# All two-operand additions and subtractions of the second norm, the token combinations and the up weights on VectorE instead of partly on GpSimd

## The chip, the cores and the metric

The kernel runs on one core of a Trainium2 chip. The metric is the device time of one execution in microseconds (us). A core has five engines that each run their own queue of instructions in order: TensorE (PE in the profile, with its weight loads as PEld), VectorE (DVE), ScalarE (ACT), GpSimd (POOL) and SyncE (SP, which here issues DMAs).

## What is computed

One layer of a streaming encoder on 1088 tokens of width 1024 (1024 of a new stream, 64 of a running one). Only its end matters here:

```python
    x = x + gate1 * (jnp.concatenate([a_out, b_out], axis=-1) @ w_out)
    h2 = rms_norm(x, g_norm2) * (1 + scale2) + shift2
    x = x + gate2 * (jnp.square(jax.nn.relu(h2 @ w_up)) @ w_down)
    return x, latent_new, krope_new, s_new
```

`w_up` is 1024 x 4096, `w_down` 4096 x 1024, everything is float32.

## The kernel before, in words

Every float32 product is made of three products of rounded halves: `split(hi, lo, src, eng)` lets ACT copy `src` into a rounded `hi` and then lets `eng` compute `lo = src - hi` (line 102); `mm3` (lines 92 to 95) multiplies hi by hi, lo by hi and hi by lo. `sub` (line 105) is a subtraction on the engine named. A `split` or a `sub` costs one instruction with two operands in SBUF on the engine named.

The up and the down projection use a seven-product scheme (Strassen's) on halves of the tokens and halves of the width, so sums and differences of the token blocks `X[11]`, `X[12]`, `X[21]`, `X[22]` (128 x 4 x 544 each) and of the weight blocks are formed and split first. The 1088 tokens come in four chunks of 272 in the order `WORDER`, two halves (`HALVES`) of each of two token blocks.

The stretch that the change touches has these parts, in the order of time:

- Output projection (`main`, about 611 to 718 us): for each chunk of 272 tokens eight blocks `m` of 24 matmuls. For each `m` DVE adds the gated product to `x` (line 1323), ACT squares it (line 1330), and POOL adds the square to the chunk's sum `acc` (line 1331). The last chunk's sum is the tile `last`.
- Second norm (`norm2`, beside `main`, its last chunk beside the up projection): TensorE sums `acc` over the partitions (line 1345), DVE and POOL form the reciprocal root (lines 1348 and 1349), DVE a diagonal (line 1352), TensorE broadcasts it (line 1356), then per row block `k` DVE scales `x` (line 1362; its second operand is in PSUM) and ACT adds the shift (line 1364). After `k == 3` in the second token block, POOL subtracts `X[21]` from `X[11]` (line 1366, shown in the trace under line 105). Chunks of the first token block are split (`AH[0]` with POOL, `AH[1]` with DVE); for the second block `sums_of` forms three more sums, on POOL (lines 1262 to 1264).
- Token operands (`tokens`): `second` forms `X[22] - X[11]` into `ts` and splits it, `third` splits `X[11]`, then the operands 4, 5 and 6 are split. Four of the eight splits of `third`, and half of the sixteen for 5 and 6, have their subtraction on POOL, the others on DVE.
- Up weights (`weights`): for each of 16 column blocks `j`, `first` and `rest` form seven operands; `put(j, i, src, eng)` takes the next of ten slots, waits until the product that used it is done, and splits into it. For `j < 2` several of these, and for every `j` the seventh (`put(j, 6, ...)`), have their subtraction on POOL.
- Up projection (`up`, about 718 to 1060 us): `product(j, i, h)` runs 12 matmuls with weight operand `i` of block `j` and the half `h` of token operand `i`. Its result is copied out by ACT (line 1565) or added by DVE (line 1551); these free the PSUM bank.

`interleave` fixes by hand-written times in which order the streams are written out. When the program is built, a planner then puts the instructions of each engine in one fixed order, which need not be that of the source. On the chip each engine takes its instructions in that order, and one that waits holds up those behind it.

Of the kernel before, what the change touches and what calls it, by code (L numbers as in the profile page):

```python
# [71 lines left out]
def layer(ctx: ExitStack, tc: tile.TileContext, I, O):  # L72
# [31 lines left out]
    def sub(out, a, b, eng):  # L104
        eng.tensor_tensor(out=out, in0=a, in1=b, op=ALU.subtract)  # L105
# [1151 lines left out]
            return h, HALVES[0], ((0, 512 * h, HW, 0),)  # L1257
        return h, HALVES[1], ((0, 512 * h + HW, 512 - HW, 0), (1, SEQ + 32 * h, 32, 512 - HW))

    def sums_of(hs, eng=None):  # L1260

        POOL.tensor_tensor(out=X[21][:, :, hs], in0=X[21][:, :, hs], in1=X[22][:, :, hs], op=ALU.add)
        sub(X[12][:, :, hs], X[12][:, :, hs], X[22][:, :, hs], eng or POOL)
        POOL.tensor_tensor(out=X[12][:, :, hs], in0=X[12][:, :, hs], in1=X[11][:, :, hs], op=ALU.add)

    with ExitStack() as octx:
        ow = octx.enter_context(tc.tile_pool(reuse_waits="tile", name="ow", bufs=1))
# [12 lines left out]
        def main():  # L1280
            ld = {}

            def load(c):
                h, hs, parts = place(c)
                mx = [xw.tile([P, 4, HW], F32, name="mx") for _ in range(2)]
                for _, t0, n, o in parts:
                    SP.dma_start(mx[0][:, :, o:o + n], mix_d[:, 0:4, t0:t0 + n])
                    SP.dma_start(mx[1][:, :, o:o + n], mix_d[:, 4:8, t0:t0 + n])
                ld[c] = mx

            def load_x(c):
                h, hs, _ = place(c)
                for b in range(2):
                    tc.keep_in_program_order(SP.dma_start(
                        X[10 * (h + 1) + 1 + b][:, :, hs],
                        I["xo_T"][512 * b:512 * b + 512, c * HW:(c + 1) * HW].rearrange("(k p) n -> p k n", p=P)))

            for w, c in enumerate(WORDER):
                _, _, parts = place(c)
                if w == 0:  # L1300
                    mh, ml = mixh[1]
                else:
                    mx = ld.pop(c)
                    mh, ml = mix_pair() if w == 2 else [xw.tile([P, 8, HW], F32R, name=f"m{x}1", bufs=1) for x in "hl"]
                    split(mh[:, 0:4], ml[:, 0:4], mx[0], DVE)
                    split(mh[:, 4:8], ml[:, 4:8], mx[1], DVE)
                load_x(c)
                if w + 1 < 4:
                    load(WORDER[w + 1])
                acc = last[:, 0:HW] if w == 3 else nw.tile([P, HW], F32, name="acc")  # L1310
                for m in range(8):
                    yield 600, 0, has(f"wo {m}")
                    if w == 0 and m < len(early):
                        po = early[m]
                    else:
                        po = (g_bank if w == 0 and m < 6 else mm_bank)()[:, 0:HW]
                        for kt in range(KT):
                            n, o = wo_place(m, kt)
                            mm3(po, wo[n][0][:, o], wo[n][1][:, o], mh[:, kt], ml[:, kt], kt == 0, kt == KT - 1)
                            yield 340, 0, None  # L1320
                    x2 = rows_of(c, m)
                    for s, _, n, o in parts:
                        DVE.scalar_tensor_tensor(out=x2[:, o:o + n], in0=po[:, o:o + n], scalar=modT[:, 2, m, s:s + 1],
                                                 in1=x2[:, o:o + n], op0=ALU.mult, op1=ALU.add)
                    SP.dma_start(x2_d[:, m, c * HW:(c + 1) * HW], x2)
                    if m == 0:
                        ACT.activation(acc, x2, AF.Square)
                    else:
                        sq = nw.tile([P, HW], F32, name="sq", bufs=3)
                        ACT.activation(sq, x2, AF.Square)  # L1330
                        POOL.tensor_tensor(out=acc, in0=acc, in1=sq, op=ALU.add)
                sums[c] = acc
                done.add(f"x2 {c}")

        def norm2():
            for c in WORDER:
                h, hs, parts = place(c)
                end = c == WORDER[-1]
                yield 0, 0, has("up" if end else f"x2 {c}")
                yield 0, 2500, None  # L1340
                acc = sums.pop(c)
                blocks = ((0, P), (P, P), (2 * P, HW - 2 * P))
                pm = tp_bank()
                for j, (o, n) in enumerate(blocks):
                    PE.matmul(pm[:n, j:j + 1], lhsT=acc[:, o:o + n], rhs=ones[:, 0:1], start=True, stop=True)
                st = last[:, 272:275] if end else nw.tile([P, 3], F32, name="st")
                for a, b, n in ((0, 2, P), (2, 3, blocks[2][1])):
                    DVE.tensor_scalar(out=st[:n, a:b], in0=pm[:n, a:b], scalar1=1.0 / D, scalar2=EPS, op0=ALU.mult, op1=ALU.add)
                    POOL.tensor_tensor(out=st[:n, a:b], in0=st[:n, a:b], in1=mhalf[:n, 0:b - a], op=ALU.pow)
                dg = last[:, 288:672].rearrange("p (j t) -> p j t", j=3) if end else nw.tile([P, 3, P], F32, name="dg", bufs=1)  # L1350
                for j, (o, n) in enumerate(blocks):
                    DVE.tensor_scalar(out=dg[:n, j, :n], in0=ident[:n, :n], scalar1=st[:n, j:j + 1], scalar2=None, op0=ALU.mult)
                yield 0, 3000, None
                bc = tp_bank()
                for j, (o, n) in enumerate(blocks):
                    PE.matmul(bc[:, o:o + n], lhsT=ones[:n, :], rhs=dg[:n, j, :n], start=True, stop=True)
                yield 600, 300, None
                for k in range(8):
                    x = rows_of(c, k)
                    for s, _, n, o in parts:  # L1360
                        xs = x[:, o:o + n]
                        DVE.scalar_tensor_tensor(out=xs, in0=xs, scalar=G12[:, 1, k, s:s + 1], in1=bc[:, o:o + n],
                                                 op0=ALU.mult, op1=ALU.mult)
                        ACT.activation(xs, xs, AF.Identity, bias=modT[:, 3, k, s:s + 1])
                    if h == 1 and k == 3:
                        sub(X[11][:, :, hs], X[11][:, :, hs], X[21][:, :, hs], POOL)
                if h == 0:
                    split(AH[0][:, :, hs], AL[0][:, :, hs], X[11][:, :, hs], POOL)
                    split(AH[1][:, :, hs], AL[1][:, :, hs], X[12][:, :, hs], DVE)
                elif not end:  # L1370
                    sums_of(hs)
            done.add("norm2")
# [15 lines left out]
    with ExitStack() as uctx:  # L1388
# [27 lines left out]
        def tokens():  # L1416
# [11 lines left out]

            def third(h, cs):
                for k in range(4):  # L1430
                    part(3, X[11][:, k, cs], k, cs, POOL if k % 2 or False else DVE)
                yield 0, 500, None
                done.add(f"tokens 3 {h}")

# [2 lines left out]
            yield 0, 500, has("third 1", "norm2")  # L1437
            yield from second(1, HALVES[1])
            yield from third(1, HALVES[1])
            sums_of(HALVES[1], DVE)  # L1440
            AL[4] = keep.tile([P, 4, HT], F32R, name="al4", tag="x11")
            for j, x in ((4, 22), (5, 21), (6, 12)):
                for h, cs in enumerate(HALVES):
                    for k in range(4):
                        part(j, X[x][:, k, cs], k, cs, POOL if j > 4 and (k + h) % 2 else DVE)
                    done.add(f"tokens {j} {h}")
                    yield 0, 500, None
                if j < 6:
                    AL[j + 1] = apool.tile([P, 4, HT], F32R, name=f"al{j + 1}", tag=f"x{x}")
                else:  # L1450
                    more = keep.tile([P, 4, 4, P], F32R, name="wq_more", tag=f"x{x}")
                    slots.extend(((more[:, 0], more[:, 1]), (more[:, 2], more[:, 3])))
# [5 lines left out]
        def weights():  # L1458
# [11 lines left out]
            def first(j):  # L1470
# [3 lines left out]
                    raws[f] = t[:, 0:4], t[:, 4:8]  # L1474
                yield 0, 2500, None
                warr[j] = {}
                yield from put(j, 0, raws[j][0], POOL if j < 2 else DVE)
                yield from put(j, 1, raws[j][1], DVE)

            def rest(j):  # L1480
                (b11, b21), (b12, b22) = raws.pop(j), raws.pop(j + 16)
                t2 = tq.tile([P, 512], F32, name="tw").rearrange("p (k n) -> p k n", k=4)
                sub(b11, b12, b11, DVE)
                sub(t2, b22, b11, POOL if j < 2 else DVE)
                yield from put(j, 2, t2, DVE)
                yield 0, 1500, None
                if j >= 2:
                    yield from put(j, 5, b11, DVE)
                    yield 0, 1500, None
                sub(b12, b22, b12, DVE)  # L1490
                yield from put(j, 3, b12, POOL if j < 2 else DVE)
                done.add(f"third {j}")
                yield 0, 1500, None
                if j < 2:
# [1 line left out]
                sub(t2, b21, t2, DVE)  # L1496
                yield from put(j, 4, t2, DVE)
                yield 0, 1500, None
                yield from put(j, 6, b22, POOL)
                yield 0, 1500, None  # L1500

            yield from first(0)
# [340 lines left out]
```

## Time and profile before

| | us |
|---|---|
| median of 3 runs | 1420.18 (1418.73 to 1422.01) |
| the profiled execution, its own time | 1419.29 |
| span of that profile | 1417.5 |
| PE busy | 1349.8 (95% of the span) |
| DVE busy | 873.6 (62%) |
| ACT busy | 655.6 (46%) |
| POOL busy | 273.1 (19%) |

Busy time of an engine is a mean over very different stretches, so the rows further down are taken by stretch. In the rows of groups the number after the bar is the busy time of the group and the mean of one instruction in ns, and after the second bar the idle time in front of it and what ended it. In a timeline, a row gives its start, its length, the engine, the line, and in brackets the idle time before it; several neighbouring instructions of one kind are merged into one row (x8), and lengths of neighbours overlap a little, since an instruction ends after the next has begun. The granted clock is 1.00 where TensorE runs at 2.4 GHz and 0.50 at 1.2 GHz.

### The profile page before, as it was taken

How to read it: one execution, taken by the hardware profiler on the slowest of the kernel's cores; microseconds unless marked ns; L12 is line 12 of the kernel's file. 1: busy time of each engine (PE TensorE's matmuls, PEld its weight loads, DVE VectorE, ACT ScalarE, POOL GpSimd, SP SyncE). 2: the span in 40 equal slices, each digit the busy share in tenths (PEclk: the TensorE clock that was granted, in tenths of full speed). 3: DMA queues.
4: the chain of work that ended last, by engine and by line, in shares of the span. 5: the costliest groups of instructions: out<-in, count | busy, mean ns of one | idle time of the engine just before them, and what ended most of it. 6: DMA issues, size and time to landing. Idle time of an engine off the chain costs nothing.

```text
span 1417.5 us, 26453 instructions
## 1 busy us (share of the span) xinstructions
PE 1349.8 (95%) x10014; PEld 1263.6 (89%) x10014; DVE 873.6 (62%) x1894; ACT 655.6 (46%) x1623; POOL 273.1 (19%) x388
## 2 busy tenths in 40 slices
PE   6988899988999999999987999999999999999998
PEld 5888788886866778899986999999999999999998
DVE  5678777336455665654489665665544776774554
ACT  5455454335335566653455544444444333333332
POOL 3155445213121211013564000000000000000000
PEclk9999999999999999999998999999999999999999
DMA  9320021384243442164224534444437864533440
GB/s 347 109 72 9 16 72 55 107 235 129 84 142 123 157 120 71 44 204 135 80 76 125 182 132 140 156 140 131 141 113 271 324 221 152 185 114 108 127 126 33
DMA packets 165594, 188.17 MB, mean 133 GB/s; under 512 B 16814, under 2 KB 116442, under 8 KB 165466
## 3 DMA queue, kind: packets, MB, share of 16 engines
q1 hardware_dynamic: 158010, 180.90, 40.0%
q10 hardware_dynamic: 7456, 5.57, 1.2%
q8 instruction: 79, 1.29, 0.4%
q14 instruction: 49, 0.40, 0.1%
HBM read 132.97 MB, written 53.46 MB: 132 GB/s over the span
## 4 chain that ended last, share of the span: by engine, by line
PE 77%; DVE 10%; DMA 4%; POOL 3%; ACT 3%; issue 2%; SPq 0%; DVEq 0%; POOLq 0%; ACTq 0%
PE mm L93 13%; PE mm L94 13%; PE mm L95 13%; PE g L93 6%; PE g L95 6%; PE g L94 5%; PE mm L964 3%; PE tp L93 3%; PE tp L95 3%; PE tp L94 3%; PE g L991 2%; PE mm L166 2%; DMA raw<-in_w_in 1%; PE tp L1001 1%; DMA gv<-mix_d 1%
## 5 line engine op out<-in xcount | busy, mean ns | idle before, releaser
L101 ACT CAST opers<-quad 128x512 fp32r<-128x512 f32 x112 | 69.4, 620 | 184.6 <-PE mm L95 145.3
L102 DVE TENSOR_TENSOR opers<-quad,opers 128x512 fp32r<-128x512 f32 x112 | 77.1, 689 | 112.6 <-ACT opers L101 112.6
L93 PE MATMUL mm<-ah,wh 128*128 128x272 f32 x424 | 123.0, 291 | 6.2 <-ACT st L1565 6.2
L93 PE MATMUL mm<-opers 128*128 128x272 f32 x448 | 128.6, 287 | 0.3 <-DVE e L1775 0.3
L95 PE MATMUL mm<-opers 128*128 128x272 f32 x448 | 128.9, 288 | 0.0
L94 PE MATMUL mm<-opers 128*128 128x272 f32 x448 | 128.3, 286 | 0.0
L95 PE MATMUL mm<-ah,wl 128*128 128x272 f32 x424 | 122.7, 290 | 1.0 <-POOL wl L102 1.0
L94 PE MATMUL mm<-al,wh 128*128 128x272 f32 x424 | 122.8, 290 | 0.0
L93 PE MATMUL mm<-hh,wh 128*128 128x384 f32 (+2 forms) x264 | 90.6, 346 | 0.6 <-ACT hh L101 0.5
L94 PE MATMUL mm<-hl,wh 128*128 128x384 f32 (+2 forms) x264 | 87.6, 333 | 0.0
L95 PE MATMUL mm<-hh,wl 128*128 128x384 f32 (+2 forms) x264 | 87.2, 331 | 0.0
L93 PEld LDWEIGHTS mm<-ah,wh 128*128 128x128 f32 x424 | 81.2, 192 | 6.5 <-ACT st L1565 6.4
L93 PEld LDWEIGHTS mm<-opers 128*128 128x128 f32 x448 | 84.6, 189 | 0.5 <-issue 0.5
L95 PEld LDWEIGHTS mm<-opers 128*128 128x128 f32 x448 | 84.3, 188 | 0.0
L94 PEld LDWEIGHTS mm<-opers 128*128 128x128 f32 x448 | 84.1, 188 | 0.0
L95 PEld LDWEIGHTS mm<-ah,wl 128*128 128x128 f32 x424 | 80.7, 191 | 1.2 <-POOL wl L102 1.2
L94 PEld LDWEIGHTS mm<-al,wh 128*128 128x128 f32 x424 | 80.9, 191 | 0.0
L102 DVE TENSOR_TENSOR opers<-ru,opers 128x544 fp32r<-128x544 f32 x108 | 77.5, 719 | 2.2 <-ACT opers L101 2.0
L101 ACT CAST opers<-ru 128x544 fp32r<-128x544 f32 x108 | 69.3, 643 | 13.1 <-PE mm L95 11.7
L101 ACT CAST wh<-ru 128x512 fp32r<-128x512 f32 x67 | 41.1, 618 | 70.9 <-PE g L94 26.0
L93 PE MATMUL mm<-wh,hh 128*128 128x264 f32 (+3 forms) x216 | 66.4, 307 | 1.6 <-ACT wh L213 1.6
L94 PE MATMUL mm<-wl,hh 128*128 128x264 f32 (+3 forms) x216 | 65.6, 304 | 0.9 <-DVE wl L105 0.9
(415 smaller groups left out, 4434.6 us busy)
## 6 DMA issues: line engine op xcount, KB each, us to landing
ru<-u_d SPq DMA_DIRECT2D x108, 272.0 KB, 2.8
raw<-in_w_ada SPq DMA_DIRECT2D x40, 512.0 KB, 3.9
ru<-in_w_up SPq DMA_DIRECT2D x32, 512.0 KB, 4.1
quad<-in_w_down SPq DMA_DIRECT2D x16, 1024.0 KB, 7.6
u_d<-st SPq DMA_DIRECT2D x60, 272.0 KB, 2.1
u_d<-sc SPq DMA_DIRECT2D x45, 272.0 KB, 2.2
raw<-in_w_in SPq DMA_DIRECT2D x22, 256.0 KB, 3.0
x<-in_xo_T SPq DMA_DIRECT2D x8, 544.0 KB, 5.1
```

The lines of the kernel that those rows point to most:

```text
L93: PE.matmul(out, lhsT=ah, rhs=bh, start=first, stop=False, skip_group_check=more)
L94: PE.matmul(out, lhsT=ah, rhs=bl, start=False, stop=False, skip_group_check=more)
L95: PE.matmul(out, lhsT=al, rhs=bh, start=False, stop=last, skip_group_check=more)
L101: ACT.copy(hi, src)
L102: eng.tensor_tensor(out=lo, in0=src, in1=f32(hi), op=ALU.subtract)
L166: mm = PE.matmul(acc[32 * j:32 * j + 32, 0:256], lhsT=scT[:, k, :], rhs=was[k][:, 256 * j:256 * (j + 1)], start=(k == 0), stop=(k == KT - ...
L964: PE.matmul(sp[:n, :w], lhsT=x[:, hd, :n], rhs=y[:, hd, :w], start=(j == 0), stop=(j == 4))
L991: PE.matmul(op[:n, 0:P], lhsT=pt[:kw, k, :n], rhs=kvs[kt // 4].v[:kw, kt % 4, hd], start=(kt == 0), stop=(kt == nkt - 1))
L1001: PE.transpose(tp[:kw, k, :n], pr[k0 // 4][:n, P * k:P * k + kw], ident[:n, :n])
```

## The change

Every addition or subtraction of two SBUF operands named above runs on DVE: 71 instructions. Nothing else is edited; what each computes, its operands and its shapes stay. POOL keeps line 1349 in this stretch.

| moved to DVE | shape | count |
|---|---|---|
| `acc` sums (line 1331) | 128x272 | 28 |
| low halves of `AH[0]`, three sums of `sums_of`, `X[11] - X[21]` | 128x1088 | 9 |
| low halves of token operands 3, 5, 6 | 128x272 | 12 |
| low halves and differences of up weights | 128x512 | 22 |

```diff
-    def sums_of(hs, eng=None):
-
-        POOL.tensor_tensor(out=X[21][:, :, hs], in0=X[21][:, :, hs], in1=X[22][:, :, hs], op=ALU.add)
-        sub(X[12][:, :, hs], X[12][:, :, hs], X[22][:, :, hs], eng or POOL)
-        POOL.tensor_tensor(out=X[12][:, :, hs], in0=X[12][:, :, hs], in1=X[11][:, :, hs], op=ALU.add)
+    def sums_of(hs):
+
+        DVE.tensor_tensor(out=X[21][:, :, hs], in0=X[21][:, :, hs], in1=X[22][:, :, hs], op=ALU.add)
+        sub(X[12][:, :, hs], X[12][:, :, hs], X[22][:, :, hs], DVE)
+        DVE.tensor_tensor(out=X[12][:, :, hs], in0=X[12][:, :, hs], in1=X[11][:, :, hs], op=ALU.add)
...
-                        POOL.tensor_tensor(out=acc, in0=acc, in1=sq, op=ALU.add)
+                        DVE.tensor_tensor(out=acc, in0=acc, in1=sq, op=ALU.add)
...
-                        sub(X[11][:, :, hs], X[11][:, :, hs], X[21][:, :, hs], POOL)
+                        sub(X[11][:, :, hs], X[11][:, :, hs], X[21][:, :, hs], DVE)
                 if h == 0:
-                    split(AH[0][:, :, hs], AL[0][:, :, hs], X[11][:, :, hs], POOL)
+                    split(AH[0][:, :, hs], AL[0][:, :, hs], X[11][:, :, hs], DVE)
...
-                    part(3, X[11][:, k, cs], k, cs, POOL if k % 2 or False else DVE)
+                    part(3, X[11][:, k, cs], k, cs, DVE)
...
-            sums_of(HALVES[1], DVE)
+            sums_of(HALVES[1])
...
-                        part(j, X[x][:, k, cs], k, cs, POOL if j > 4 and (k + h) % 2 else DVE)
+                        part(j, X[x][:, k, cs], k, cs, DVE)
...
-                yield from put(j, 0, raws[j][0], POOL if j < 2 else DVE)
+                yield from put(j, 0, raws[j][0], DVE)
...
-                sub(t2, b22, b11, POOL if j < 2 else DVE)
+                sub(t2, b22, b11, DVE)
...
-                yield from put(j, 3, b12, POOL if j < 2 else DVE)
+                yield from put(j, 3, b12, DVE)
...
-                yield from put(j, 6, b22, POOL)
+                yield from put(j, 6, b22, DVE)
```

## Rows read from the trace of the kernel before

**Rows 1.** Busy time by stretch: the stretch in us, its length, then for PE, PEld, DVE, ACT and POOL the busy us and in brackets the instructions, the granted clock, the DMA share and GB/s.

```profile
640.00:700.00 60.00, 59.77 (x470) 58.80 (x468) 27.21 (x65) 20.49 (x40) 29.97 (x26) 1.00 0.39 117
711.50:764.00 52.50, 40.86 (x284) 39.11 (x284) 48.83 (x81) 31.11 (x85) 33.43 (x27) 0.90 0.20 57
...
752.00:754.00 2.00, 2.00 (x11) 2.00 (x10) 2.00 (x5) 2.00 (x6) 1.42 (x2) 0.50 0.00 0
...
758.00:760.00 2.00, 2.00 (x18) 2.00 (x17) 2.00 (x3) 0.39 (x1) 2.00 (x3) 1.00 0.55 138
...
800.00:820.00 20.00, 20.00 (x162) 20.00 (x161) 11.92 (x21) 9.10 (x18) 1.29 (x1) 1.00 0.44 147
```

**Rows 2.** What TensorE waited for between 700 and 800 us: line, releaser, us in total, times, longest.

```profile
PE mm L93 <- ACT st L1565: 6.2, 1, 6.2
PE g L93 <- DVE st L1551: 2.8, 2, 2.1
PE tp L1345 <- POOL last L1331: 2.4, 1, 2.4
```

**Rows 3.** Timeline of TensorE: the first matmul after its longest wait.

```profile
751.20 0.59 PE L93 MATMUL mm<-ah,wh 128*128 128x272 f32 x1 [6.20 <-ACT st L1565]
```

**Rows 4.** Groups of DVE instructions between 711.5 and 764 us, different shapes kept apart.

```profile
L102 DVE TENSOR_TENSOR al<-x,ah 128x272 fp32r<-128x272 f32 x20 | 12.0, 654 | 0.0
L105 DVE TENSOR_TENSOR ts<-x,x 128x272 f32<-128x272 f32 x8 | 7.7, 1004 | 1.0 <-POOL x L105 1.0
L102 DVE TENSOR_TENSOR al<-ts,ah 128x272 fp32r<-128x272 f32 x8 | 6.7, 860 | 0.0
L105 DVE TENSOR_TENSOR ru<-ru 128x512 f32<-128x512 f32 x4 | 4.5, 1124 | 0.3 <-DMA ru<-in_w_up 0.3
L102 DVE TENSOR_TENSOR wl<-ru,wh 128x512 fp32r<-128x512 f32 x4 | 4.0, 1008 | 1.1 <-ACT wh L101 1.1
...
L102 DVE TENSOR_TENSOR wl<-tw,wh 128x512 fp32r<-128x512 f32 x3 | 3.1, 1047 | 0.1
...
L1352 DVE TENSOR_SCALAR last<-ident,last 128x128 f32<-128x128 f32 x2 | 1.8, 940 | 0.0
```

**Rows 5.** The same DVE operations with POOL idle beside them: timeline rows (a run of two and a run of eight 128x272, one 128x1088, one 128x512), and one group of the whole stretch 620 to 1080 us (the 128x128 diagonal of the chunks before the last).

```profile
748.85 0.78 DVE L102 TENSOR_TENSOR al<-ts,ah 128x272 fp32r<-128x272 f32 x2
749.55 2.89 DVE L102 TENSOR_TENSOR al<-x,ah 128x272 fp32r<-128x272 f32 x8
...
742.08 1.28 DVE L105 TENSOR_TENSOR x<-x,x 128x1088 f32<-128x1088 f32 x1
...
781.01 0.69 DVE L105 TENSOR_TENSOR tw<-ru 128x512 f32<-128x512 f32 x1
...
L1352 DVE TENSOR_SCALAR dg<-ident,st 128x128 f32<-128x128 f32 x6 | 1.4, 283 | 2.3 <-POOL st L1349 2.3
```

**Rows 6.** Timelines of DVE and of POOL from 733 to 760 us, rows that stand beside each other in time.

```profile
733.35 4.35 DVE L1362 SCALAR_TENSOR_TENSOR x<-x,G,tp 128x240 f32<-128x240 f32 x16 [0.17 <-PE tp L1356]
736.43 2.55 POOL L105 TENSOR_TENSOR x<-x,x 128x1088 f32<-128x1088 f32 x1 [4.07 <-ACT x L1364]
739.01 3.15 DVE L105 TENSOR_TENSOR ts<-x,x 128x272 f32<-128x272 f32 x2 [0.96 <-POOL x L105]
739.16 2.70 POOL L1262 TENSOR_TENSOR x<-x,x 128x1088 f32<-128x1088 f32 x1 [0.18 <-ACT x L1364]
752.72 3.69 DVE L102 TENSOR_TENSOR al<-x,ah 128x272 fp32r<-128x272 f32 x4
752.58 3.53 POOL L102 TENSOR_TENSOR al<-x,ah 128x272 fp32r<-128x272 f32 x4 [5.01 <-issue]
```

**Rows 7.** Timelines of DVE and POOL in the output projection: a POOL sum of 128x1088, and DVE's line 1323 inside it (128x240 and 128x32).

```profile
679.31 2.54 POOL L1262 TENSOR_TENSOR x<-x,x 128x1088 f32<-128x1088 f32 x1
680.55 0.63 DVE L1323 SCALAR_TENSOR_TENSOR x<-mm,modT,x 128x240 f32<-128x240 f32 x2 [2.35 <-PE mm L95]
```

**Rows 8.** Groups of POOL instructions between 711.5 and 764 us (left out: line 1264, one like line 1262, and line 1349, which stays on POOL).

```profile
L102 POOL TENSOR_TENSOR al<-x,ah 128x272 fp32r<-128x272 f32 x12 | 11.1, 948 | 7.8 <-issue 5.0 <-ACT ah L101 2.3 <-ACT wh L101 0.5
L102 POOL TENSOR_TENSOR wl<-ru,wh 128x512 fp32r<-128x512 f32 x5 | 7.4, 1491 | 0.8 <-ACT wh L101 0.8
L105 POOL TENSOR_TENSOR tw<-ru 128x512 f32<-128x512 f32 x2 | 3.0, 1511 | 1.6 <-DVE ru L105 1.6
L1331 POOL TENSOR_TENSOR last<-last,sq 128x272 f32<-128x272 f32 x3 | 2.7, 914 | 1.4 <-PE mm L95 1.1 <-ACT sq L1330 0.2
L1262 POOL TENSOR_TENSOR x<-x,x 128x1088 f32<-128x1088 f32 x1 | 2.7, 2697 | 0.2 <-ACT x L1364 0.2
...
L105 POOL TENSOR_TENSOR x<-x,x 128x1088 f32<-128x1088 f32 x1 | 2.6, 2552 | 4.1 <-ACT x L1364 4.1
```

**Rows 9.** Timeline of DVE in 764 to 780 us, the two two-operand instructions that lasted longest.

```profile
766.01 1.37 DVE L102 TENSOR_TENSOR wl<-ru,wh 128x512 fp32r<-128x512 f32 x1 [0.64 <-ACT wh L101]
774.29 1.80 DVE L105 TENSOR_TENSOR st<-sc,st 128x544 f32<-128x544 f32 x1
```

**Rows 10.** Timelines of DVE and POOL around the seventh weight split of one block of the up projection.

```profile
793.75 0.69 DVE L102 TENSOR_TENSOR wq_more<-tw,wq_more 128x512 fp32r<-128x512 f32 x1 [2.31 <-ACT wq_more L101]
796.80 1.29 POOL L102 TENSOR_TENSOR wq_more<-ru,wq_more 128x512 fp32r<-128x512 f32 x1 [21.29 <-ACT wq_more L101]
798.12 0.44 DVE L1551 TENSOR_TENSOR st<-st,g 128x272 f32<-128x272 f32 x1 [3.68 <-ACT st L1565]
```

## The prediction

> **What bounds the kernel now.** Read busy time by stretch first, not over the span. In the output projection TensorE works 59.77 of 60 us, and in the up projection proper 20.00 of 20; DVE works 45% and 60% there, so it has room [rows 1]. Between the two, from 711.5 to 764 us, the picture turns: DVE is busy 48.83 of 52.5 us, TensorE 40.86 at a granted clock of 0.90 [rows 1]. That stretch is where the last chunk's norm, the token operands and the first weights are made, and it is bound by DVE. The table of TensorE's waits shows the cost: 6.2 us for an ACT copy, 2.4 us for POOL's last sum of squares, 2.8 us for DVE's additions [rows 2]. After the longest wait TensorE starts at 751.20 us [rows 3], and at 752 us its granted clock is 0.50, the 1.2 GHz level: 11 matmuls in 2 us, where 18 run at 758 us [rows 1]. So the change is worth what it does to DVE's queue between 711.5 and about 775 us.
>
> **How much POOL costs DVE there.** Lay the groups of DVE in this stretch beside the same operations with POOL idle. For 128x272 the idle-POOL length follows from two runs: two take 0.78 and eight take 2.89 us [rows 5], so each further one adds (2.89 - 0.78)/6 = 0.35 us and one alone lasts 0.43. In the stretch the means are 654, 1004 and 860 ns [rows 4]. The excess is 20 x 0.226 = 4.5, 8 x 0.576 = 4.6 and 8 x 0.432 = 3.5 us. For 128x512, 0.69 us alone [rows 5], it is 4 x 0.43 = 1.7, 4 x 0.32 = 1.3 and 3 x 0.355 = 1.1 us [rows 4]; for the two diagonals 2 x (0.940 - 0.283) = 1.3 us [rows 4, 5]. Together 18.0 us of DVE's 48.8 are excess. The timelines side by side show its cause: DVE's two `ts` subtractions take 3.15 us, starting with a POOL sum of 2.70 us, and four subtractions on each engine take 3.69 us together [rows 6]. Eight on DVE alone took 2.89 [rows 5]: the shared work is slower than DVE by itself.
>
> The Trainium skill, SBUF — State Buffer, Who interferes with whom, says that a DVE instruction with two SBUF inputs and a GpSimd one that reads SBUF exclude each other for a whole instruction, and that a DVE instruction with at most one SBUF input, outside some modes, does not suffer. The trace agrees with both: the 3.15 us above, and DVE's line 1323, one operand in PSUM, keeps 0.63 us for its two inside POOL's sum [rows 6, 7].
>
> **The change part by part.** It moves 71 instructions: 31 before 711.5 us, 25 from there to 764, 2 up to 780, and 13 later (one per block).
>
> 711.5 to 764 us. POOL's groups give twelve and three of 128x272, five and two of 128x512 and, with line 1264, three of 128x1088 [rows 8]. In DVE's queue each costs its length less the 0.08 us by which neighbours overlap (0.43 - 0.35): 15 x 0.35 + 7 x 0.61 + 3 x 1.20 = 13.1 us, the last from 1.28 us alone [rows 5]. DVE gives up 18.0 and takes on 13.1: 4.9 us less. It also no longer waits 0.96 us for POOL's `X[11] - X[21]` [rows 6]: 5.9.
>
> 764 to 780 us. Two DVE instructions of 1.37 and 1.80 us [rows 9] shrink to about 0.69 and 0.74 (the second a little longer than 128x512): 1.7 less; two splits of 0.61 come in: 0.5 us gained. Sum 6.4.
>
> New waits. An instruction moved into DVE's queue holds up what is behind it. (a) `X[11] - X[21]` is written after the first eight of the sixteen instructions of line 1362. DVE would reach it at 733.35 + 4.35/2 = 735.5, ACT's shifts let it go at 736.43 [rows 6]: 0.9 us, with the other eight queued behind; nothing if the planner sets it after all sixteen. I take 0.9. (b) Five low halves of weights wait for ACT's copy: DVE's own seven waited 1.1 + 0.1 us [rows 4], 0.17 each: 0.9 us. (c) The last sum of squares waits for ACT's square; POOL waited 1.4 us before its three [rows 8], so 0.5 us for the one that ends the chain. Together 2.3 us. Bounds: none at all; or all the 8.1 us that POOL waited for ACT in this stretch (2.3 + 0.5 + 0.8 + 0.2 + 0.2 + 4.1) [rows 8] falls to DVE. The middle value stands nearest to DVE's own row, whose subtractions of tokens show no idle time before them [rows 4].
>
> Output projection. 25 sums of squares at 0.35 and six 128x1088 at 1.20 add 16 us over 90 us to an engine that is busy 27.21 of 60 [rows 1]. Queued behind them are line 1323's additions, which free TensorE's banks. They wait 2.35 us for TensorE today [rows 7], and a bank is needed again only four blocks `m` later; the longest run that can stand in front is four sums, 4.8 us. Costed at nothing; without that cover, at most 4.8 - 2.35 = 2.5 us once.
>
> Up projection proper. One split of 0.61 us per block, in which DVE is busy 11.92 of 20 us [rows 1]. POOL starts it at 796.80 us, while DVE idles 3.68 us before its addition at 798.12 [rows 10]. It fits there: nothing. POOL's instruction disturbs no one there either, so nothing comes back.
>
> The moved work issues no DMA and passes none on a queue of SP; POOL keeps only line 1349.
>
> **The sum.** 6.4 - 2.3 = 4.1 us. The profiled execution took 1419.29 us (span 1417.5, and 1.8 around it), 0.9 under the median. The saving is a difference, so it is taken off the median: 1420.18 - 4.1 = 1416.1 us. Since TensorE works behind DVE in that stretch, I let DVE's saving pass through in full.
>
> **The rivals.**
>
> 1. The gain is larger: no new waits (6.4 us), and TensorE's wait before 751.20 gets so short that the clock stays up. At half clock TensorE does 11 matmuls per 2 us against 18 [rows 1]; some 6 us of that hold 33, which would take 3.7: 2.3 us more. 1420.2 - 8.7 = 1411.5 us. Against it: the wait is 6.2 us [rows 2], and DVE's saving up to there is only part of the 6.4.
>
> 2. DVE takes over POOL's waits. POOL stood before casts and shifts, at no one's cost; in one queue these waits delay tokens. At the bound of 8.1 us the sum is +1.7, 1421.9 us; with two thirds of it, -1.0; I take 1420.5. For it: ACT is also busy, 31 of 52.5 us [rows 1], and a planner that does not know the lengthened times fixes the order. Against it: DVE's own token splits show no idle time [rows 4].
>
> 3. Slower: the seventh weight split of each block is queued ahead of the additions of line 1551 at a place where its cast is late. ACT casts only when a slot is free; POOL waited 21.29 us for that [rows 10]. If the idle 3.68 us don't take it up, TensorE slips by one split, 0.69 us, in each of 13 blocks: 9.0 us, 1416.1 + 9.0 = 1425.1 us. It decides from the point where the split is queued more than 3.7 us early. Against it: DVE waits in the same way for its sixth split, 2.31 us [rows 10], and TensorE still works 20.00 of 20.
>
> 4. Nothing comes back: the excess of 18 us is not POOL's doing and stays. Then DVE, which is full, gets 13.1 + 1.2 us more: 1434.5 us. Against it: every lengthened row stands beside a POOL instruction, the short ones don't [rows 5, 6]. The Trainium skill, Perfetto Trace Analysis, Optimizing Scalar/DVE Operations, says that where DVE is saturated, moving work away, even to GpSimd, may make sense, and this change does the reverse; it adds that between these two it may not help because they share a read port. The second half is what the rows show.
>
> **How the numbers follow.** Forecast 0.48 (its own range 1413.5 to 1418.5), rival 1 0.13, rival 2 0.23, rival 3 0.12, rival 4 0.04. About 0.2%, 2.8 us, is what a measurement can tell from no change: faster is under 1417.3, slower over 1423.0. Faster: 0.44 of the forecast, all of rival 1 and 0.02 of rival 2, 0.59. Same: 0.04 and 0.20, 0.24. Slower: 0.01 of rival 2, rivals 3 and 4, 0.17. The range reaches from rival 1 a little beyond rival 2's bound, 1411.0 to 1423.5; what is left out is rival 4, most of rival 3 and the tail below.
>
> **What the profile after would show.** Right: means of DVE's 128x272 near 0.43 us and of 128x512 near 0.69 everywhere; DVE's busy time from 711.5 us to its token splits' end about 5 us shorter; TensorE's wait near 751 us shorter, its work after 780 unchanged but shifted. Wrong: DVE rows that wait for ACT casts or shifts (rival 2), TensorE waits after 780 us (rival 3), or lengths that stay (rival 4). The step least sure is the order in DVE's queue: it is not in the trace of before, and it decides how much of the 6.4 us TensorE sees.

## The result, and the profile after

| | before | after |
|---|---|---|
| median, us | 1419.45 (1417.42 to 1422.01, 4 runs) | 1407.64 (1403.91 to 1408.70, 4 runs) |
| span of the profiled run | 1417.5 | 1402.1 (its own time 1403.91) |

The ratio is 0.9911, 95% interval 0.9886 to 0.9936: about 12 us faster. Forecast were 1416.1 us and a range of 1411.0 to 1423.5. The sign and the place were right, the size was about a third of what came, and the time lies below the range.

Busy time by stretch of the kernel after. The first row is the work from 709.3 us to the end of the token splits; the columns are those of [rows 1].

```profile
709.30:756.60 47.30, 41.58 (x317) 39.92 (x316) 44.72 (x109) 35.67 (x94) 1.25 (x2) 1.00 0.23 69
620.00:700.00 80.00, 80.00 (x632) 79.20 (x631) 50.95 (x111) 29.55 (x57) 3.74 (x6) 1.00 0.39 117
800.00:820.00 20.00, 20.00 (x162) 20.00 (x161) 12.19 (x21) 9.62 (x19) 0.00 (x0) 1.00 0.46 150
```

Groups of DVE in the first of these stretches, shapes kept apart.

```profile
L102 DVE TENSOR_TENSOR al<-x,ah 128x272 fp32r<-128x272 f32 x32 | 12.1, 441 | 0.0
L102 DVE TENSOR_TENSOR wl<-ru,wh 128x512 fp32r<-128x512 f32 x10 | 6.8, 691 | 0.7 <-ACT wh L101 0.6
...
L102 DVE TENSOR_TENSOR al<-ts,ah 128x272 fp32r<-128x272 f32 x8 | 3.2, 436 | 0.0
L105 DVE TENSOR_TENSOR ts<-x,x 128x272 f32<-128x272 f32 x8 | 3.2, 438 | 0.0
...
L1352 DVE TENSOR_SCALAR last<-ident,last 128x128 f32<-128x128 f32 x2 | 0.5, 284 | 0.4 <-POOL last L1349 0.4
```

What TensorE waited for between 690 and 800 us: line, releaser, us in total, times, longest.

```profile
PE mm L93 <- ACT wh L101: 2.2, 2, 1.4
PE tp L93 <- DVE x L1362: 1.9, 1, 1.9
PE g L94 <- DVE al L102: 1.1, 1, 1.1
PE mm L93 <- ACT st L1565: 0.9, 2, 0.6
PE mm L93 <- ACT sc L1571: 0.2, 1, 0.2
```

Timeline of DVE around the subtraction that the planner set among the sixteen instructions of line 1362.

```profile
726.15 2.76 DVE L1362 SCALAR_TENSOR_TENSOR x<-x,G,tp 128x240 f32<-128x240 f32 x10 [0.17 <-PE tp L1356]
729.19 1.29 DVE L105 TENSOR_TENSOR x<-x,x 128x1088 f32<-128x1088 f32 x1 [0.28 <-ACT x L1364]
```

Every lengthened group of [rows 4] has the length that it had with POOL idle [rows 5]: `ts` fell from 1004 to 438 ns, the token splits from 654 and 860 to 441 and 436, the weights from about 1010 to 691, the diagonals from 940 to 284. DVE carries 109 instructions in the 47.3 us, against 81 in 52.5 [rows 1]. TensorE's waits are the second thing to see: the 6.2 us stop [rows 3] is gone, and so is the 2.4 us for POOL's last sum of squares; five short ones are left, 6.3 us together. The granted clock is 1.00, where it was 0.90 [rows 1].

For comparison, before: the four waits of TensorE from 690 to 800 us that [rows 2] leaves out, and the slices of 720 to 780 us, columns as in [rows 1].

```profile
PE tp L1356 <- DVE last L1352: 1.0, 1, 1.0
PE mm L95 <- POOL wl L102: 1.0, 1, 1.0
PE g L95 <- DVE wl L102: 0.8, 1, 0.8
PE g L94 <- POOL al L102: 0.3, 1, 0.3
...
720.00:740.00 20.00, 15.61 (x106) 14.76 (x105) 18.83 (x41) 14.30 (x44) 13.37 (x11) 0.91 0.03 8
740.00:760.00 20.00, 12.75 (x82) 11.89 (x81) 20.00 (x28) 11.51 (x32) 13.38 (x12) 0.83 0.06 14
760.00:780.00 20.00, 17.20 (x122) 16.66 (x122) 18.41 (x28) 10.03 (x21) 4.64 (x4) 0.91 0.70 212
```

**Where the 15.4 us between the two profiled spans went.** Two losses of TensorE can be read in every profile: its waits from 690 to 800 us, added up, and what it loses at the 1.2 GHz level, taken as 20 us times (1 less the granted clock) over each 20 us slice from 700 to 800 us. Span less both is nearly one number for all kernels in which nothing else was edited:

| kernel | span | waits | half clock | span less both |
|---|---|---|---|---|
| before | 1417.5 | 14.5 | 7.0 | 1396.0 |
| after | 1402.1 | 6.3 | 0.0 | 1395.8 |
| after, profiled again (E1) | 1406.2 | 5.9 | 3.6 | 1396.7 |
| E2 | 1423.3 | 17.3 | 8.6 | 1397.4 |
| E3 | 1408.7 | 7.5 | 5.4 | 1395.8 |
| E4 to E8 | 1406.1 to 1419.4 | 5.1 to 12.8 | 3.6 to 10.2 | 1394.3 to 1397.4 |
| E9 | 1413.8 | 11.4 | 6.8 | 1395.6 |
| E10 | 1412.8 | 10.2 | 7.0 | 1395.6 |
| E11 | 1406.1 | 7.1 | 3.4 | 1395.6 |

So nearly the whole gain is time that TensorE lost in this stretch and no longer loses. The columns are an estimate: where TensorE waits at half clock, the same time stands in both, by finer slices about 1.0 us in before, nothing in after and E1, 2.3 in E2 and 2.5 in E9. The first profile of after had no slice at half clock. E1, near the median's time, has two slices at 0.91; its two losses are 21.5 - 9.5 = 12.0 us below before's, its span is 11.3 us shorter, and the medians of before and after differ by 11.8. E1's two slices, columns as in [rows 1]:

```profile
740.00:760.00 20.00, 16.30 (x112) 15.42 (x111) 18.73 (x42) 11.17 (x26) 0.00 (x0) 0.91 0.24 71
760.00:780.00 20.00, 20.00 (x149) 20.00 (x149) 16.92 (x31) 8.38 (x16) 0.00 (x0) 0.91 0.74 254
```

The table says where the time was, not why; that is for the experiments.

### The profile page after: what moved, and what is told of

It is laid out like the page before. It is cut to its first block, busy times and chain, and to the rows that moved or that the text cites. A ratio compares the mean times of both kernels' runs of the same rounds, so it can differ in the third digit from the quotient of the medians.

```text
span 1402.1 us, 26363 instructions
## 1 busy us (share of the span) xinstructions
PE 1340.1 (96%) x10014; PEld 1254.8 (89%) x10014; DVE 890.4 (64%) x1965; ACT 656.1 (47%) x1623; POOL 183.8 (13%) x317
## 4 chain that ended last, share of the span: by engine, by line
PE 78%; DVE 10%; DMA 4%; ACT 3%; POOL 2%; issue 2%; SPq 0%; DVEq 0%; POOLq 0%; ACTq 0%
PE mm L93 13%; PE mm L94 13%; PE mm L95 13%; PE g L95 5%; PE g L93 5%; PE g L94 5%; PE mm L964 3%; PE tp L93 3%; PE tp L95 3%; PE tp L94 3%; PE g L991 2%; PE mm L166 2%; DMA raw<-in_w_in 1%; PE tp L1001 1%; DVE ST L725 1%
## 5 line engine op out<-in xcount | busy, mean ns | idle before, releaser
L101 ACT CAST opers<-ru 128x544 fp32r<-128x544 f32 x108 | 69.4, 643 | 13.1 <-PE mm L95 11.7
L102 DVE TENSOR_TENSOR wl<-ru,wh 128x512 fp32r<-128x512 f32 x67 | 46.1, 691 | 36.3 <-ACT wh L101 36.0
```

The lines of the kernel that those rows point to most:

```text
L101: ACT.copy(hi, src)
L102: eng.tensor_tensor(out=lo, in0=src, in1=f32(hi), op=ALU.subtract)
```

## The experiments

The theories. "Port": GpSimd's reading lengthens DVE's instructions with two SBUF operands, and shorter ones are the gain. Against it, "order": when the change is built, the planner also sets the queues of the other engines in another order (83 of ACT's 1623 traced instructions stand at another place, compared by line, tile and shape), and this is the gain. Later ones are named where they come in.

**E1, the changed kernel once more**, for the size.

> The changed kernel once more, as the mark for the other runs of this call. Both theories: 0.991 of the kernel before.

Measured: 1407.11 us (1406.36 to 1408.0), ratio 0.9910 [0.9897, 0.9924]. The size stands.

**E2 and E3, GpSimd kept busy beside the changed kernel.** DVE does all that it does in after; beside most of the instructions that were moved (not the low halves of `AH[0]` and two weight differences), GpSimd runs useless ones into a scratch tile. In E2 they read about as much as the old instructions did; in E3 GpSimd reads one column and fills the scratch with constants, so it is about as busy (38.8 us from 711.5 to 764 us, E2 38.1, before 33.4) but reads next to nothing. The queues of TensorE, ACT and SP are after's, row for row; in DVE's two neighbours change places. The calls of `beside` are left out here.

```diff
+    def beside(src):
+        POOL.tensor_tensor(out=out, in0=src, in1=src, op=ALU.subtract)                     # E2
+        POOL.tensor_tensor(out=shad[:, 0:1], in0=..., in1=mhalf[:, 0:1], op=ALU.subtract)  # E3
+        POOL.memset(out, 0.0); POOL.memset(out, 0.0)                                       # E3
```

> The changed kernel, with useless GpSimd subtractions put beside VectorE's: where the kernel before had its work on GpSimd, GpSimd now subtracts a tile of the same operand (ACT's rounded half, the square, the shifted rows) from itself into a scratch tile that nobody reads. VectorE still does all the work, and the queues of TensorE, ScalarE and SyncE hold the same instructions in the same order as in the changed kernel; in VectorE's queue two neighbours change places. Theory 'port' (the gain is that no two-operand instruction of VectorE stands against a GpSimd one any more): VectorE's 128x272 rows lengthen again from 0.43 us to 0.6 to 1.0 where a GpSimd instruction runs, and at least 9 of the 12 us are lost, 0.997 of the kernel before or above; it may be slower than it, since VectorE has both its own work and the waits. Theory 'order' (the gain beyond my 4 us comes from the new order in which TensorE's and ScalarE's queues are laid out): that order is kept here, so no more than the 4 to 6 us that I worked out for VectorE come back, 0.994 to 0.996.

> As the run before, but beside VectorE's work GpSimd only writes: one subtraction of a single column (to wait for the same operand) and then two fills of the scratch tile with zeros, so that it is busy about as long without reading from SBUF. Port: if it is GpSimd's reading that holds VectorE up, the rows of VectorE keep 0.43 us and the time stays at 0.991, at most 1 us more for the short column instructions. Order: the same time, 0.991. If it is slower by several us, GpSimd's mere presence costs something (its writes, or the semaphores), and the first run proves less than it seems.

Measured: E2 1424.83 us, 1.0037 [1.0024, 1.0050]; E3 1412.70 us, 0.9949 [0.9937, 0.9961]. DVE's groups from 711.5 to 775 us and its longest wait for GpSimd, E2:

```profile
L102 DVE TENSOR_TENSOR al<-x,ah 128x272 fp32r<-128x272 f32 x32 | 17.1, 592 | 0.0
...
L102 DVE TENSOR_TENSOR al<-ts,ah 128x272 fp32r<-128x272 f32 x8 | 5.7, 746 | 0.0
L105 DVE TENSOR_TENSOR ts<-x,x 128x272 f32<-128x272 f32 x8 | 4.0, 541 | 0.0
...
DVE last L1362 <- POOL last L1359: 2.8, 1, 2.8
```

and E3 from 709 to 764 us, with one of GpSimd's groups of fills and the wait of DVE for GpSimd under them:

```profile
L102 DVE TENSOR_TENSOR al<-x,ah 128x272 fp32r<-128x272 f32 x32 | 12.0, 436 | 0.0
L102 DVE TENSOR_TENSOR wl<-ru,wh 128x512 fp32r<-128x512 f32 x12 | 8.1, 687 | 2.3 <-ACT wh L101 2.2
...
L105 DVE TENSOR_TENSOR ts<-x,x 128x272 f32<-128x272 f32 x8 | 3.2, 436 | 0.0
L102 DVE TENSOR_TENSOR al<-ts,ah 128x272 fp32r<-128x272 f32 x8 | 3.2, 436 | 0.1
...
L1259 POOL MEMSET shad<- 128x272 f32 x29 | 9.4, 325 | 1.7
...
DVE last L1364 <- POOL last L1361: 2.0, 1, 2.0
```

GpSimd that only writes leaves DVE at 436 and 687 ns; GpSimd that reads lengthens the same instructions of 128x272 to 541 to 746 ns.

E2 and E3 differ in what GpSimd reads (and in how many instructions it runs for that), and by 12.1 us; DVE's stretch, from TensorE's last output projection matmul to the last token split, is 52.4 us in E2 and 40.9 in E3. So GpSimd's reads lengthen DVE, and they cost as much as the whole gain of the change. "Order" alone falls: with after's order E2 is slower than before.

Two limits remain. The 12.1 us hold some lateness of GpSimd itself, since the reciprocal root (POOL's one remaining step of the norm chain) stands behind the useless reads and the diagonal waits 2.8 us for it. And E3 misses its forecast of at most 1 us more: it is 5.6 us behind after. There the root stands behind the fills, and the diagonal waits 2.0 us for it where after waits 0.4; that this makes the 5.6 us is likely but not shown. E3's expectation says what follows for such a case, that E2 proves less than it seems: of the 17.7 us by which E2 lies above E1, 12.1 go with the reading, and 5.6 with something that E3 has too.

**E4 to E6 and E8, one part alone.** The other instructions stay on GpSimd. One line of each edit is shown.

```diff
-                yield from put(j, 0, raws[j][0], POOL if j < 2 else DVE)   # E4: the six weight instructions of j < 2
+                yield from put(j, 0, raws[j][0], DVE)
-        POOL.tensor_tensor(out=X[21][:, :, hs], ...)                       # E5: the nine 128x1088
+        DVE.tensor_tensor(out=X[21][:, :, hs], ...)
-                    part(3, X[11][:, k, cs], k, cs, POOL if k % 2 or False else DVE)   # E6: the twelve token splits
+                    part(3, X[11][:, k, cs], k, cs, DVE)
-                        POOL.tensor_tensor(out=acc, in0=acc, in1=sq, op=ALU.add)       # E8: the 28 sums of squares
+                        DVE.tensor_tensor(out=acc, in0=acc, in1=sq, op=ALU.add)
```

> The kernel before with only six of the 71 instructions moved to VectorE: the splits 0 and 3 and the difference of the first two weight blocks. Port: they are 6 of the 25 in the stretch, 3.7 us of VectorE's time against about a fifth to a quarter of the 18 us of lengthening; the gain is 0 to 3 us, 0.998 to 1.000. Order: this edit alone changes ScalarE's queue most of the way to that of the changed kernel, so it should bring a large part of the 8 us that I did not forecast, 0.993 to 0.996.

> The kernel before with only the nine 128x1088 instructions moved to VectorE (the low half of AH0, X11 - X21 and the three sums of sums_of). Theory 'sum': each part gives what its GpSimd time lengthens VectorE less its own time there; these are 8 of the 32 us of GpSimd work in the stretch, so 18 x 8/32 - 3.6 = 0.9 us, with the 0.96 us wait some 2 us: 0.997 to 1.000. Theory 'stop': TensorE's 6.2 us wait and the half clock after it come from the two differences ts, which stand against the big GpSimd sums (3.15 and 3.67 us for two instead of 0.78), hold up ScalarE's casts and with them the copy that frees the bank; with the big sums gone the wait falls under 3 us, and the gain is 5 to 9 us: 0.9935 to 0.9965.

> The kernel before with only the twelve low halves of the token operands 3, 5 and 6 moved. Sum: 11.1 of the 32 us of GpSimd work, 18 x 11/32 - 12 x 0.35 = 2.0 us, 0.997 to 1.000. Stop: these run after the wait for the most part (10 of the 12), so the 6.2 us stay and the gain is 1 to 3 us, 0.998 to 0.9995. The two differ only in whether the 6.2 us wait stays, which they both allow here; the run is for the size of the part.

> The kernel before with only the 28 sums of squares (line 1331) moved. Both theories: three of the 28 lie in the stretch where VectorE is full, and the last of them stood behind two weight splits in GpSimd's queue (719.4 to 722.8 us); with it on VectorE TensorE's wait of 2.4 us for it can shrink: gain 0 to 3 us, 0.998 to 1.000. In the output projection VectorE takes on 25 x 0.35 us; if that is not free, as I took it to be, this run is slower than the kernel before, 1.001 to 1.003.

| run | median, us | ratio, 95% interval |
|---|---|---|
| E4 weights | 1417.88 | 0.9991 [0.9981, 1.0001] |
| E5 128x1088 | 1414.66 | 0.9961 [0.9945, 0.9976] |
| E6 tokens | 1416.49 | 0.9980 [0.9969, 0.9991] |
| E8 sums | 1418.96 | 1.0000 [0.9989, 1.0012] |

The parts give 0.9, 3.9, 2.0 and 0 thousandths, 6.8 together against 9 for all (the seventh splits alone were not run). E4 was meant to test "order" too, and does not: its ACT queue differs from after's at 75 places, hardly fewer than before's 83. While some GpSimd reads are left, they fall beside whatever DVE then does: in E4 the eight `ts` (711.5 to 764 us) became longer than before.

```profile
L105 DVE TENSOR_TENSOR ts<-x,x 128x272 f32<-128x272 f32 x8 | 9.6, 1226 | 0.0
```

In E6 it was GpSimd that starved. Timelines of GpSimd and of DVE:

```profile
753.16 8.74 POOL L102 TENSOR_TENSOR wl<-ru,wh 128x512 fp32r<-128x512 f32 x2 [3.90 <-ACT wh L101]
...
752.72 2.90 DVE L102 TENSOR_TENSOR al<-x,ah 128x272 fp32r<-128x272 f32 x8
755.54 0.68 DVE L102 TENSOR_TENSOR wl<-tw,wh 128x512 fp32r<-128x512 f32 x1
756.14 2.89 DVE L102 TENSOR_TENSOR al<-x,ah 128x272 fp32r<-128x272 f32 x8
```

**E7, all but the nine 128x1088.** After E5 I thought that the 128x1088 were what removed the long stop ("stop"), against "sum": the parts add up and are worth what DVE saves.

> The changed kernel with the nine 128x1088 instructions back on GpSimd. Sum: it loses the 2 us of that part, 0.992 to 0.994. Stop: the big sums stand against the differences again, TensorE's wait of some 6 us and the half clock come back, 0.996 to 0.999.

Measured: 1408.34 us, 0.9916 [0.9899, 0.9932]. "Stop" falls. "Sum" is met within the interval here, but moving the 128x1088 is worth 5.5 us alone (E5) and nothing measurable once the rest is moved. E7's waits add up to 5.1 us, though two `ts` still last 3.11 us beside POOL. The parts are not additive.

**E9 and E10, only DVE made longer.** The changed kernel with useless subtractions of 128x272 among DVE's token splits; GpSimd reads as little as in after. This prices a microsecond of DVE in this stretch. The expectations count eight and sixteen, but the edited function serves five operands and two halves, and the traces show ten in E9 and twenty in E10: at 0.35 us each 3.5 and 7.0 us of DVE, not 2.8 and 5.6.

```diff
                 split(AH[j][:, k, cs], AL[j][:, k, cs], x, eng)
+                if k == 1:        # E10: if k % 2
+                    DVE.tensor_tensor(out=shad, in0=x, in1=x, op=ALU.subtract)
```

> The changed kernel with eight useless subtractions of 128x272 in DVE's queue among its token splits (line 1419, row block k = 1 of each half and operand; they write to a scratch tile that nobody reads). GpSimd reads nothing beside them. At 0.35 us each they take 2.8 us of DVE in the stretch after the output projection. Theory 'passes through once': TensorE ends 2.8 us later, 1407.4 + 2.8 = 1410.2 us (ratio 0.993 to 0.994). Theory 'stops and half clock': a microsecond of DVE costs TensorE more than itself, since it makes stops longer and takes the clock down behind them; by the difference of the two traces (5.2 us of DVE for 12 us) 2.3 times, 1407.4 + 6.5 = 1413.9 us (ratio 0.996). Theory 'reading itself': DVE's time in that stretch has slack, the loss came from GpSimd's reads alone: 1407 to 1408 us (0.991).

> The same with sixteen useless subtractions (odd row blocks k), 5.6 us of DVE, a little more than the 5.2 us by which this stretch of DVE's work got shorter with the change. 'Passes through once': 1413.0 us (ratio 0.9953 to 0.996). 'Stops and half clock': 1419 to 1421 us (ratio 1.0), and TensorE's waits plus its half-clock loss in 690 to 800 us back at 18 to 22 us. 'Reading itself': 1407 to 1408 us (0.991). In all cases the span less TensorE's waits and half-clock loss of 690 to 800 us stays within 1394 to 1398 us if nothing else moved.

Measured: E9 1414.39 us, 0.9964 [0.9952, 0.9976]; E10 1415.32 us, 0.9977 [0.9966, 0.9988]. TensorE's waits from 690 to 800 us, E9:

```profile
PE g L95 <- DVE wl L102: 5.1, 1, 5.1
PE g L94 <- DVE al L102: 3.4, 2, 2.4
PE tp L93 <- DVE x L1363: 2.5, 1, 2.5
PE tp L1346 <- DVE last L1332: 0.4, 1, 0.4
```

E10:

```profile
PE tp L93 <- DVE wl L102: 3.7, 1, 3.7
PE tp L93 <- DVE x L1363: 3.6, 1, 3.6
PE g L94 <- DVE al L102: 2.6, 1, 2.6
PE mm L93 <- ACT wh L101: 0.3, 1, 0.3
```

and the slices of E10 from 720 to 780 us, columns as in [rows 1]:

```profile
720.00:740.00 20.00, 16.28 (x114) 15.62 (x113) 18.49 (x53) 17.16 (x53) 1.25 (x2) 0.91 0.01 2
740.00:760.00 20.00, 14.84 (x99) 13.90 (x97) 20.00 (x49) 6.89 (x18) 0.00 (x0) 0.91 0.09 26
760.00:780.00 20.00, 18.54 (x129) 18.55 (x130) 17.25 (x33) 12.78 (x24) 0.00 (x0) 0.83 0.67 213
```

The ten cost 7.3 us (1414.39 - 1407.11), the twenty 8.2. With the true counts "passes through once" gives 1410.9 and 1414.4 us: E9 misses it clearly, E10 by 0.9 us only. "Reading itself" is missed in both: with no more reads of GpSimd than in after, DVE's length alone brings back two thirds of the loss. The fixed factor of 2.3 is near E9 (7.3/3.5 = 2.1) and missed by E10 (8.2/7.0 = 1.2), so it is no factor; that the place of the work in the queue decides which stops arise fits the two lists of waits, and is not tested by itself. In E9 one 5.1 us wait for a weight split makes most of it. DVE's stretch, taken as under E2 and E3, is 37.2 us in after, 39.8 in E9 and 42.8 in E10; before it was 42.3. So E10 has before's length of DVE and yet is 4 us faster (1415.32 against 1419.39 us): its waits are 10.2 us against 14.5, and it has none of those for POOL itself, 2.4 us for the last sum [rows 2] and 1.0 and 0.3 for a weight and a token split.

**E11, tokens, weights and seventh splits moved, sums and 128x1088 left on GpSimd.**

> Only the token, weight and seventh splits on DVE; the 28 sums of squares and the nine 128x1088 stay on GpSimd. Those 37 had gained little when they alone were moved (nothing, and 0.4 per cent) and nothing when the nine were put back. 'Sum': 1408 to 1412 us (0.992 to 0.995), no better than the changed kernel. If DVE's freed 5 us of own work in the stretch were worth more than the reading of the three 128x1088 and three sums that fall into it: 1404 to 1406 us (0.989 to 0.990), better than both.

Measured: 1410.46 us, 0.9933 [0.9920, 0.9947]. "Sum" holds; taking 5 us of its own work off DVE in the stretch gave nothing, and TensorE again waits 1.7 us for POOL's last sum. DVE's stretch is 41.6 us, 4.4 longer than after's, and costs 3.4 us against E1.

**E12, the first stage too.** There GpSimd's splits of `h` and of the first weights (lines 482 and 309) stand beside a full DVE at 70 to 90 us.

```diff
-        LO = ((DVE, POOL), (POOL, POOL))
+        LO = ((DVE, DVE), (DVE, DVE))
...
-                        split(h["h"][:, k, c0:c0 + cn], h["l"][:, k, c0:c0 + cn], hf[:, k, c0:c0 + cn], POOL)
+                        split(h["h"][:, k, c0:c0 + cn], h["l"][:, k, c0:c0 + cn], hf[:, k, c0:c0 + cn], DVE)
```

> The changed kernel, and in the first stage too the low halves of h (line 482, 12 subtractions) and of the first weight groups (line 309, 6) on DVE instead of GpSimd. In 80 to 90 us DVE is full (10.00 of 10) and TensorE at 7.47 of 10 while GpSimd reads beside DVE, so the same picture in small. If the mechanism holds there: 1 to 3 us less than the changed kernel, 1404.5 to 1406.5 us (0.989 to 0.9905). If DVE's longer queue decides there: 1409 to 1412 us (0.993 to 0.995).

Measured: 1403.10 us (1402.49 to 1406.61), 0.9887 [0.9873, 0.9901], the best of all and a little below its expected range (1404.5 to 1406.5 us); against E1 the difference is 4 us by medians, with intervals that overlap a little. Slice 80 to 90 us and one group of DVE, after:

```profile
80.00:90.00 10.00, 7.47 (x54) 6.83 (x53) 10.00 (x25) 7.69 (x21) 3.40 (x4) 1.00 0.37 108
...
L476 DVE TENSOR_SCALAR hf<-hf,modT 128x384 f32<-128x384 f32 x8 | 5.5, 717 | 0.0
```

and E12:

```profile
80.00:90.00 10.00, 10.00 (x81) 9.98 (x80) 9.79 (x29) 7.40 (x20) 0.00 (x0) 1.00 0.40 108
...
L476 DVE TENSOR_SCALAR hf<-hf,modT 128x384 f32<-128x384 f32 x8 | 3.3, 414 | 0.0
```

TensorE's 2.5 idle us there are gone, and span less both losses of the later stretch is 1401.8 - 4.8 - 3.6 = 1393.4, 2.4 below the table's 1395.8: this agrees with the mechanism found above, at a place where it was looked for.

## Why the prediction was right or wrong

- **What bounds the kernel**, right: nearly the whole gain lies between 690 and 800 us, in TensorE's waits and its clock.
- **POOL's reads lengthen DVE**, right, and now shown: E2 against E3. The 18.0 us of excess came back in full; the groups after have the lengths that the prediction read with POOL idle. The rule of the Trainium skill (SBUF — State Buffer, Who interferes with whom), that a GpSimd instruction that only writes does not contend with a DVE instruction of two SBUF inputs, was not tested by before's trace; E3 agrees with it, 436 ns.
- **DVE's own sum**, right, a little too small. From the end of TensorE's last output projection matmul (718.4 us before, 716.2 after) to the end of the last token split (760.7 and 753.4), DVE's stretch fell from 42.3 to 37.2 us, 5.1 less. Worked out up to 764 us were 4.9 and 0.96, less 2.3 us of new waits: 3.6.
- **New waits**, a little too dear: 0.28 for 0.9 at the subtraction, 0.6 for 0.9 at the weights, 0.5 for 0.5 at the sums (there by luck: of the 1.4 us that it was taken from, 1.1 were a wait for TensorE, not for ACT's square [rows 8]). Rival 2 (DVE takes POOL's waits) did not come.
- **"I let DVE's saving pass through in full"**, wrong; this is the step that failed. It takes the stretch for one chain in which TensorE runs DVE's length and nothing more. TensorE's lost time fell by 12.0 us (E1) to 15.2 us (the first profile of after) for 5.1 us of DVE. In reverse, E9 and E10 lengthen DVE's stretch by 2.6 and 5.6 us and cost 7.3 and 8.2. Nor is there another fixed rate: E11's 4.4 us cost 3.4, and the 11.5 us between E2 and E3 cost 12.1. What the lists of waits show instead is that TensorE stops separately at several operands that come late (a copy, a weight, a sum of squares, a normed row): 14.5 us of waits became 6.3 (E1 5.9), and the loss at half clock 7.0 us before became 0 to 3.6 after. Of the waits that went, 3.7 us were for POOL's own late results (2.4, 1.0 and 0.3); the sum, which counts DVE's time alone, has no term for them, though it lists the 2.4. Rival 1 had the clock in it, but priced one stop and 2.3 us, and was taken as unlikely because DVE's saving up to 751.20 us was "only part of the 6.4".
- **Output projection costed at nothing**, right: TensorE works 80.00 of 80 us while DVE rises to 50.95; E8 alone changes nothing. **Seventh split in the up projection**, right: 20.00 of 20, DVE 12.19 of 20, where it had 11.92 [rows 1]; rival 3 did not come. Rival 4 is excluded by the lengths.

What stays open: what sets the rate, and with it why the ten subtractions of E9 cost nearly as much as the twenty of E10. E9 and E10 are also set in order anew by the planner, so that their stops fall at different operands; a kernel that keeps after's order and only stretches DVE was not made. Nor was before's own order without GpSimd's reads. About 2 us of the difference between the first two profiled spans arose before the end of the output projection (718.4 and 716.2 us); E1, which is after's kernel, ends it at 717.9, so most of this is scatter.

## What to carry to other kernels

When DVE is full and GpSimd reads SBUF beside its two-operand instructions, compare the length of each DVE group with the same group while GpSimd is idle; the excess against the cost of moving GpSimd's work over says whether to move it, and here 18.0 against 13.1 us was enough. Do not pass the saving of a feeding engine to TensorE one to one: list all of TensorE's waits in that stretch and the slices below full clock; their sum (here 21.5 us, of which about 12 came back) is an estimate of the most that can come back there. And measure the parts together: left-over reads fall beside other instructions, and the parts do not add up (the 128x1088 were worth 5.5 us alone and nothing on top of the rest).

## What the runs showed of the hardware that was not expected

- Back-to-back DVE instructions with two SBUF operands can lock GpSimd out: two of its 128x512, 1.3 to 1.5 us each elsewhere [rows 8, 10], took 8.74 us in E6 while DVE kept the lengths that it has with GpSimd idle (eight 128x272 in 2.90 us). In E2 one read of GpSimd that took 0.83 us just before lasted 5.15, beside DVE rows of such lengths. Elsewhere DVE was the one slowed. Which engine pays changed from place to place.

```profile
717.56 0.83 POOL L1257 TENSOR_TENSOR shad<-sq 128x272 f32<-128x272 f32 x1 [2.35 <-ACT sq L1339]
721.35 5.15 POOL L1257 TENSOR_TENSOR shad<-sq 128x272 f32<-128x272 f32 x1 [2.96 <-ACT sq L1339]
```

- A DVE instruction with one SBUF tensor can suffer too: the TENSOR_SCALAR of line 476, 32-bit, took 717 ns beside GpSimd's splits and 414 without (E12), and the prediction's own diagonals are of this kind, 940 and 283 ns [rows 4, 5]. The prediction's rule on one SBUF input has the words "outside some modes"; the Trainium skill (SBUF — State Buffer, Who interferes with whom) names `tensor_scalar` among the operations that can enter such modes. The trace agrees with that exception.
- Half clock scatters from run to run with the same kernel: the granted clock from 740 to 780 us was 1.00 in one profile of after and 0.91 in the next, about 3.6 us of their 4.1 us difference in span.
